# Two heads on the two column halves of TensorE: values held, probabilities streamed, and the division by the row sums put ahead of the transposes

## The chip, the cores and the metric

The kernel runs on one core of one Trainium2 chip. The metric is the device time of one execution in microseconds (us), where lower is better. The kernel before took 1848.61 us in the median of three runs (1846.76 to 1851.04).

## The reference, cut to what matters

The program is a stack of transformer layers on 256 tokens of width 1024: a mixer of stick-breaking and sparse attention ("even"), a conv-gated feed-forward layer, "forgetting" attention ("fox"), a second feed-forward layer, then a recurrent mixer and dilated attention ("dl") with feed-forward layers around them. All of it is float32. The change touches the last two products of the three attention stages. For fox, per head of width 64 and per block of 128 queries, they are:

```
s = jnp.einsum('bqhd,bshd->bhqs', qb, k, preferred_element_type=jnp.float32) * scale
s = s + (cq[..., :, None] - cum[..., None, :])
p = masked_softmax(s, kpos[None, :] <= tpos[:, None])
return jnp.einsum('bhqs,bshd->bqhd', p.astype(v.dtype), v)
```

The outputs of all 16 heads then stand side by side and are multiplied by an output matrix. In the sparse half of the even stage two such results (and a third over 15 compressed blocks) are added with a gate each; in the dilated stage three groups of keys share one softmax of 512 columns for each half of the tokens; in stick-breaking attention the weights come from a running product and aren't divided by a sum.

## The kernel before, in words

The three attention stages are the functions `even`, `fox` and `dilated`. Each projects its inputs with TensorE products of split operands (an fp32r high part and an fp32r low part, three products for each piece, lines 321 to 325), runs the heads in pairs, and multiplies the result by the output weights (`wout`). A pair of heads (j, with a = 0, 1) sits in one tile of 128 rows, head a in rows 64a to 64a+63.

The path of a pair, in fox: `scores` (line 555) makes the scores of both heads on TensorE, K = 64 rows each, head 0 in the upper and head 1 in the lower half of the rows. `softmax` takes the maximum (VectorE, lines 577 and 579) and the exponential with its row sum (ScalarE, line 594). `transpose_p` (line 598) turns the 128x128 blocks of probabilities on TensorE (line 604) into the PSUM tile `ps_PT`, and ScalarE copies them to the SBUF tile `PT` (line 606). `pv` (line 609) multiplies: the turned probabilities `PT` are the stationary operand (128x128), the values `v0`, `v1` (the two blocks of 128 keys) are the moving one (64 columns). The result `o` (`ps_o`) has queries on its partitions, two halves of tokens by two heads of 64 columns. `scale_out` (line 615) divides by the row sums while it copies `o` to `on` (line 622), and `heads_out` (line 625) turns `on` back with two TensorE transposes (line 630), because the output product wants channels on the partitions, and splits it into `oH` and `oL` (lines 634 and 635).

The even stage does the same without `scale_out`: its sparse half (`weigh` and `mix`, lines 809 and 824) has already scaled the probabilities (line 821), its stick-breaking half (`stick_a` and `stick_b`, lines 868 and 888) has nothing to divide by, and both copy `o` with ScalarE (lines 839 and 907). The dilated stage has its own `weigh` (line 1322) and `mix` (line 1346): per pair and half of the tokens, four blocks of keys for each head, so eight transposes (line 1351), two copies (line 1353) and eight products.

In the profile a float32 product stands as two MATMULs and two weight loads, called passes here; a transpose or an fp32r product is one. So the 200 products on `vN` and 48 on `vs` are 400 and 96 passes.

The order in which the stages ask for work is written out in the strings EVD, FXD and DLD (`w` weighs a pair, `m` mixes it; `x` and `y` in the even stage). Within that, the tile framework's scheduler gives each engine a fixed order when the kernel is built, and fills TensorE's gaps with projection products (`g` pieces, all named `ps_mm`). TensorE works through its list in that order. The scores have two PSUM banks (three in dl), the turned probabilities two, `o` one.

Of the kernel before, what the change touches and what calls it, by code (L numbers as in the profile page):

```python
# [9 lines left out]
F32 = mybir.dt.float32  # L10
# [3 lines left out]
AF = mybir.ActivationFunctionType  # L14
ALU = mybir.AluOpType
AX = mybir.AxisListType
P = 128
# [178 lines left out]
class Net:  # L196
# [411 lines left out]

    def pv(self, o, v0, v1, PT, first):

        k = {"skip_group_check": True}
        self.mm(o[:, 1], PT[:, 256:384], v0, start=first, stop=False, **k)
        self.mm(o[:, 1], PT[:, 0:128], v1, start=False, **k)
        self.mm(o[:, 0], PT[:, 128:256], v0, start=False, **k)

    def scale_out(self, o, sm, H, L, rev=False):
        nc = self.nc
        rs = self.sp.tile([P, 2, 2], F32, name="rs2")
        nc.vector.reciprocal(rs[:], sm[:])
        on = self.ap.tile([P, 2, P], F32, name="on")  # L620
        v = lambda z: z.rearrange("p t (a d) -> p (t a) d", d=64)
        nc.vector.tensor_mul(v(on[:]), v(o), rs[:].rearrange("p t a -> p (t a)")[:, :, None].to_broadcast([P, 4, 64]))
        self.heads_out(on, H, L, rev)

    def heads_out(self, on, H, L, rev=False):

        nc = self.nc
        p = self.psum((P, T), "PT")
        for tt in range(2):
            nc.tensor.transpose(p[:, tt * P:(tt + 1) * P], on[:, tt], self.ident[:])  # L630
        if rev:
            H, L = (z.rearrange("p (n t) -> p t n", t=2)[:, :, ::-1] for z in (H, L))
            p = p.rearrange("p (t n) -> p t n", t=2)
        nc.scalar.copy(H, p)
        nc.vector.tensor_sub(L, p, H.bitcast(F32))


    def even(self, done):
        nc, tc = self.nc, self.tc
        with ExitStack() as ctx:  # L640
# [168 lines left out]
            def weigh(j, b):  # L809

                rows = [slice(64 * a, 64 * a + 64) for a in range(2)]
                Sl = self.scores([qr[j // 2][r, j % 2, :] for r in rows], [kkr[r, b, :] for r in rows])
                sm = self.sp.tile([P, 2, 2], F32, name="sm2")
                ABs = self.softmax(Sl, [K["cmask"], K["cmask"]], 0.125, sm)
                rs = self.sp.tile([P, 2, 2], F32, name="rs2")
                nc.vector.reciprocal(rs[:], sm[:])
                nc.vector.tensor_mul(rs[:], rs[:], gview[:, :, j::4, 1 + b])
                for a in range(2):
                    for tt in range(2):
                        v = ABs[a][1 - tt]  # L820
                        nc.vector.tensor_scalar(v, v, rs[:, tt, a:a + 1], None, ALU.mult)
                NS[j, b] = ABs

            def mix(j, b):
                if b == 0:
                    NO[0] = self.psum((P, 2, P), "o")
                o, ABs = NO[0], NS.pop((j, b))
                for a in range(2):
                    PT = self.transpose_p(ABs[a])
                    s = slice(128 * b + 64 * a, 128 * b + 64 * a + 64)  # L830
                    self.pv(o[:, :, 64 * a:64 * a + 64], vs[:, 0, s], vs[:, 1, s], PT, a + b == 0)
                if b == 0:
                    return
                rr = slice(64 * (j % 2), 64 * (j % 2) + 64)
                for tt in range(2):
# [51 lines left out]

            def stick_b(u, j, a):
                utri, nones = K["utri"], K["nones"]
                if a == 0:  # L890
                    NO[0] = self.psum((P, 2, P), "o")
                o = NO[0]
# [6 lines left out]
                aT = ap.tile([P, 384], F32, name="PT", bufs=4)  # L899
                nc.scalar.activation(aT[:], Zv, AF.Exp)  # L900
                h = slice((2 * j + a) * 64, (2 * j + a) * 64 + 64)
                self.pv(o[:, :, 64 * a:64 * a + 64], vN[:, 0, h], vN[:, 1, h], aT, a == 0)
                if a == 0:
                    return
                c = 2 * u + j
                on = ap.tile([P, 2, P], F32, name="on")
                nc.scalar.copy(on[:], o)
                self.heads_out(on, oH[:, c, :], oL[:, c, :])

            E = {}  # L910
            qr = [None, None]
# [32 lines left out]
    def fox(self, done):  # L944
        nc, tc = self.nc, self.tc
        with ExitStack() as ctx:
# [40 lines left out]
            def weigh(u, j, qT, kT, e):  # L987
# [7 lines left out]
                e[:] = [self.softmax(Sl, [cmask, cmask], 0.125, sm), sm]  # L995

            def mix(u, j, vN, e):
                ABs, sm = e
                o = self.psum((P, 2, P), "o")
                for a in range(2):  # L1000
                    PT = self.transpose_p(ABs[a])
# [240 lines left out]
    def dilated(self, kH, kL, Rkv, done):  # L1242
        nc, tc = self.nc, self.tc
        with ExitStack() as ctx:
# [77 lines left out]
            def weigh(u, G, bias, j, t, sm):  # L1322

                two = lambda z: z.rearrange("p (b n) -> p b n", b=2)
                S = [self.psum((P, 512), "S") for _ in range(2)]
                for g, c, n in ((0, 0, 256), (1, 256, P), (2, 384, P)):
                    for a in range(2):
                        q, k = (G[g][i][64 * a:64 * a + 64, j, :] for i in range(2))
                        self.mm(S[a][:, c:c + n], q[:, t * P:t * P + P], k if g == 0 else k[:, t * P:t * P + P])
                Pt = ap.tile([P, 2, 512], F32, name="Pt")  # L1330
# [8 lines left out]
                                                       ALU.max, mx[:, a, i:i + 1])  # L1339
                nm = self.sp.tile([P, 2], F32, name="nmj")  # L1340
                nc.vector.tensor_reduce(nm[:], mx[:], AX.X, ALU.max, negate=True)
                for a in range(2):
                    nc.scalar.activation(Pt[:, a], Pt[:, a], AF.Exp, bias=nm[:, a:a + 1], accum_out=sm[:, t, a:a + 1])
                return Pt

            def mix(v, Pt, j, t, o):
                for a in range(2):
                    s = slice((2 * j + a) * 64, (2 * j + a) * 64 + 64)
                    pp = self.psum((P, 4, P), "PT")
                    for i in range(4):  # L1350
                        nc.tensor.transpose(pp[:, i], Pt[:, a, i * P:(i + 1) * P], self.ident[:])  # L1351
                    PT = ap.tile([P, 4, P], F32, name="PT", bufs=3)
                    nc.scalar.copy(PT[:], pp)
                    for i, val in enumerate((v[0][:, 0, s], v[0][:, 1, s], v[1][:, t, s], v[2][:, t, s])):
                        self.mm(o[:, t, 64 * a:64 * a + 64], PT[:, i], val, start=a + t + i == 0, stop=False,
                                skip_group_check=True)

            B = {}
            its, heads = DLD.split(), True
            for i, it in enumerate(its):  # L1360
# [15 lines left out]
                    B[("T",) + w] = turn(B.pop(("r",) + w), w[1])  # L1376
                elif n == "w":
                    u, jj, t = w
                    if t == 0:
                        B["m", u, jj] = self.sp.tile([P, 2, 2], F32, name="sm2")  # L1380
                    G = [B["T", u, g] for g in range(3)]
                    B[("p",) + w] = weigh(u, G, B["b", u], jj, t, B["m", u, jj])
                else:
                    u, jj, t = w
                    if t == 0:
                        o = self.psum((P, 2, P), "o")
                    mix([B["v", u, g] for g in range(3)], B.pop(("p",) + w), jj, t, o)
                    if t == 1:
                        self.scale_out(o, B["m", u, jj], oH[:, 2 * u + jj, :], oL[:, 2 * u + jj, :], rev=True)
            self.wout("dl", oH, oL, done)  # L1390

    def bias_scratch(self, cp, R=None):
# [201 lines left out]
```

## Time and profile before

| what | value |
|---|---|
| median of three runs | 1848.61 us |
| the profiled execution | 1848.29 us |
| its span, from the first to the last instruction | 1846.5 us |
| TensorE busy, share of the span | 99% |
| VectorE busy | 69% |
| ScalarE busy | 56% |
| granted TensorE clock, mean | 0.998 |

The profile is of one execution; a line number in it is that of the kernel file above. PE is TensorE's matmuls, PEld its weight loads, DVE is VectorE, ACT is ScalarE. [...]

### The profile page before, as it was taken

What the parts mean: (1) busy time and instruction counts of PE and PEld (TensorE: products, weight loads), DVE (VectorE), ACT (ScalarE), POOL (GpSimd) and SP (SyncE); (2) the same over time, 40 slices, a digit from 0 to 9 for tenths busy, and PEclk for the clock granted to TensorE, in tenths of its full rate; (3) what the DMA queues carried; (4) which work ended last, traced back from release to release, by engine and by line L of the source; (5) the groups of instructions that cost most, each with busy time, mean ns of one, the idle gap of its engine ahead of it and who ended that gap; (6) DMA issues with size and microseconds to landing.
All of it is one profiled execution on the core that took longest, in us unless ns stands there. A gap on an engine that the chain in (4) does not pass through costs nothing.

```text
span 1846.5 us, 37819 instructions
## 1 busy us (share of the span) xinstructions
PE 1826.5 (99%) x15709; PEld 1792.6 (97%) x15709; DVE 1268.5 (69%) x2695; ACT 1041.6 (56%) x2167; POOL 3.9 (0%) x18
## 2 busy tenths in 40 slices
PE   8999999999999999999999999999999999999999
PEld 7989999999999999999999999999999999999999
DVE  6557986654888687668988766866666456458763
ACT  5556665555666565556766554645456556556542
POOL 0000000000000000000000000000000000000000
PEclk9999999999999999999999999999999999999999
DMA  7313555641565546554335555555564434426553
GB/s 251 120 41 137 199 204 192 192 148 61 184 221 197 196 171 218 180 207 167 119 111 197 208 191 190 202 191 192 189 219 143 165 124 151 138 92 218 194 188 109
DMA packets 61160, 314.72 MB, mean 170 GB/s; under 512 B 10459, under 2 KB 21115, under 8 KB 28348
## 3 DMA queue, kind: packets, MB, share of 16 engines
q1 hardware_dynamic: 45792, 305.16, 46.7%
q10 hardware_dynamic: 15196, 7.15, 1.4%
q8 instruction: 123, 2.02, 0.4%
q14 instruction: 49, 0.40, 0.1%
HBM read 311.17 MB, written 1.11 MB: 169 GB/s over the span
## 4 chain that ended last, share of the span: by engine, by line
PE 95%; DVE 2%; ACT 1%; DMA 1%; issue 0%; SPq 0%; ACTq 0%
PE ps_mm L321 21%; PE ps_mm L324 21%; PE ps_mm L325 21%; PE ps_mm L293 6%; PE ps_mm L292 6%; PE ps_mm L294 6%; PE ps_S L332 4%; PE ps_o L332 4%; DMA raw<-in_wall_dram 1%; PE ps_PT L1351 1%; DVE wL L274 1%; PE ps_PT L332 1%; PE ps_PT L604 0%; PE ps_PT L1298 0%; ACT wH L273 0%; PE ps_PT L630 0%
## 5 line engine op out<-in xcount | busy, mean ns | idle before, releaser
L273 ACT CAST wH<-raw 128x512 fp32r<-128x512 f32 (+1 forms) x1212 | 651.5, 598 | 499.9 <-PE ps_mm L324 232.8
L274 DVE TENSOR_TENSOR wL<-raw,wH 128x512 fp32r<-128x512 f32 (+1 forms) x1212 | 755.4, 663 | 253.4 <-ACT wH L273 251.6
L321 PE MATMUL ps_mm<-xH,wH 128*128 128x256 f32 x2568 | 713.1, 278 | 8.8 <-ACT xH L343 7.0
L325 PE MATMUL ps_mm<-xH,wL 128*128 128x256 f32 x2560 | 711.7, 278 | 0.0
L324 PE MATMUL ps_mm<-xL,wH 128*128 128x256 f32 x2560 | 710.8, 278 | 0.2
L321 PEld LDWEIGHTS ps_mm<-xH,wH 128*128 128x128 f32 x2568 | 483.8, 189 | 10.5 <-ACT xH L343 7.0
L324 PEld LDWEIGHTS ps_mm<-xL,wH 128*128 128x128 f32 x2560 | 482.8, 189 | 0.8 <-DVE xL L344 0.7
L325 PEld LDWEIGHTS ps_mm<-xH,wL 128*128 128x128 f32 x2560 | 482.7, 189 | 0.7 <-DVE wL L274 0.3
L294 PE MATMUL ps_mm<-hH,wL 128*128 128x256 f32 x1056 | 291.5, 276 | 0.0
L292 PE MATMUL ps_mm<-hH,wH 128*128 128x256 f32 x1056 | 291.5, 276 | 0.0
L293 PE MATMUL ps_mm<-hL,wH 128*128 128x256 f32 x1056 | 291.5, 276 | 0.0
L293 PEld LDWEIGHTS ps_mm<-hL,wH 128*128 128x128 f32 x1056 | 198.2, 188 | 0.0
L294 PEld LDWEIGHTS ps_mm<-hH,wL 128*128 128x128 f32 x1056 | 198.2, 188 | 0.0
L292 PEld LDWEIGHTS ps_mm<-hH,wH 128*128 128x128 f32 x1056 | 198.2, 188 | 0.0
L321 PE MATMUL ps_mm<-wH,kH 128*128 128x256 f32 (+1 forms) x390 | 108.1, 279 | 0.0
L324 PE MATMUL ps_mm<-wL,kH 128*128 128x256 f32 x384 | 107.2, 279 | 0.0
L325 PE MATMUL ps_mm<-wH,kL 128*128 128x256 f32 x384 | 106.7, 278 | 0.0
L321 PE MATMUL ps_mm<-wH,xH 128*128 128x256 f32 (+1 forms) x372 | 104.2, 282 | 0.0
L324 PE MATMUL ps_mm<-wL,xH 128*128 128x256 f32 x368 | 103.5, 281 | 0.0
L325 PE MATMUL ps_mm<-wH,xL 128*128 128x256 f32 x368 | 103.4, 281 | 0.0
L503 DVE TENSOR_TENSOR t<-ps_mm,R 128x512 f32<-128x512 f32 x66 | 45.5, 690 | 74.1 <-PE ps_mm L325 74.0
L321 PEld LDWEIGHTS ps_mm<-wH,kH 128*128 128x128 f32 x390 | 72.9, 188 | 0.0
(295 smaller groups left out, 2247.9 us busy)
## 6 DMA issues: line engine op xcount, KB each, us to landing
raw<-in_wall_dram SPq DMA_DIRECT2D x254, 1024.0 KB, 4.8
raw<-in_wall_dram SPq DMA_DIRECT2D x40, 768.0 KB, 4.3
raw<-in_wall_dram SPq DMA_DIRECT2D x8, 512.0 KB, 3.3
bt<-scr ACTq DMA_DIRECT2D x8, 258.0 KB, 5.6
bt<-scr ACTq DMA_DIRECT2D x4, 512.0 KB, 6.7
x<-in_xin_dram SPq DMA_DIRECT2D x4, 256.0 KB, 5.4
raw<-in_wall_dram SPq DMA_DIRECT2D x4, 256.0 KB, 5.6
cw<-in_cmpw_dram ACTq DMA_DIRECT2D x1, 1024.0 KB
```

The source lines that it names most:

```text
L273: self.nc.scalar.copy(H[:, s], raw[:, s])
L274: self.nc.vector.tensor_sub(L[:, s], raw[:, s], H[:, s].bitcast(F32))
L292: nc.tensor.matmul(out, A[0], B[0], start=start, stop=False)
L293: nc.tensor.matmul(out, A[0], B[1], start=False, stop=False)
L294: nc.tensor.matmul(out, A[1], B[0], start=False, stop=stop)
L321: nc.tensor.matmul(out[:, j, at:at + n], A[0], B[0][:, at:at + n], start=c == c0 and j == 0, stop=False, **k)
L324: nc.tensor.matmul(out[:, j, :], A[0], B[1], start=False, stop=False, **k)
L325: nc.tensor.matmul(out[:, j, :], A[1], B[0], start=False, stop=c == c1 - 1, **k)
L332: self.nc.tensor.matmul(out, l, r, start=start, stop=stop, **k)
L503: nc.vector.tensor_mul(t2[:], u, Rb)
L1351: nc.tensor.transpose(pp[:, i], Pt[:, a, i * P:(i + 1) * P], self.ident[:])
```

## The change

`pv` swaps the operands: the values of one head (128 keys by 64 columns) are now stationary, and the turned probabilities (256 or 128 queries) move. The result `o` has channels on its partitions, head 0 on partitions 0 to 63 and head 1 on 64 to 127, so that the two heads use the two halves of TensorE's columns, and their products stand alternately in the program. `o` needs no turning back: `scale_out` and `heads_out` go, and `pair_out` splits `o` straight into `oH` and `oL`. Queries are no longer on the partitions of `o`, so the division by the sums moves to the probabilities: `scaled` in fox (four VectorE operations for each pair), two operations and a reciprocal of its own for each `weigh` in dl. `mix` turns both heads before it multiplies. In the scores the second head is asked first.

```diff
     def scores(self, q, k, extra=None):
...
-            for a in range(2):
+            for a in (1, 0):
                 self.mm(S[a][:, c:c + n], q[a][:, t], k[a][:, 0:n], stop=extra is None)
...
     def pv(self, o, v0, v1, PT, first):
 
         k = {"skip_group_check": True}
-        self.mm(o[:, 1], PT[:, 256:384], v0, start=first, stop=False, **k)
-        self.mm(o[:, 1], PT[:, 0:128], v1, start=False, **k)
-        self.mm(o[:, 0], PT[:, 128:256], v0, start=False, **k)
-
-    def scale_out(self, o, sm, H, L, rev=False):
+        for v, t, c in ((v0, slice(0, 256), slice(128, 384)), (v1, slice(128, 256), slice(0, 128))):
+            for a in range(2):
+                self.mm(o[64 * a:64 * a + 64, t], v[a], PT[a][:, c], start=first and v is v0, stop=False, **k)
+
+    def scaled(self, ABs, rs):
+        for a, AB in enumerate(ABs):
+            for tt in range(2):
+                v = AB[1 - tt]
+                self.nc.vector.tensor_scalar(v, v, rs[:, tt, a:a + 1], None, ALU.mult)
+
+    def pair_out(self, p, H, L, rev=False):
         nc = self.nc
-        rs = self.sp.tile([P, 2, 2], F32, name="rs2")
-        nc.vector.reciprocal(rs[:], sm[:])
-        on = self.ap.tile([P, 2, P], F32, name="on")
-        v = lambda z: z.rearrange("p t (a d) -> p (t a) d", d=64)
-        nc.vector.tensor_mul(v(on[:]), v(o), rs[:].rearrange("p t a -> p (t a)")[:, :, None].to_broadcast([P, 4, 64]))
-        self.heads_out(on, H, L, rev)
-
-    def heads_out(self, on, H, L, rev=False):
-
-        nc = self.nc
-        p = self.psum((P, T), "PT")
-        for tt in range(2):
-            nc.tensor.transpose(p[:, tt * P:(tt + 1) * P], on[:, tt], self.ident[:])
...
             def mix(j, b):
...
                 rr = slice(64 * (j % 2), 64 * (j % 2) + 64)
-                for tt in range(2):
-                    self.mm(o[:, tt], PcT[rr, j // 2, tt * P:(tt + 1) * P], vcz[rr, :], start=False,
-                            skip_group_check=True)
-                on = ap.tile([P, 2, P], F32, name="on")
-                nc.scalar.copy(on[:], o)
-                self.heads_out(on, oH[:, 4 + j, :], oL[:, 4 + j, :])
+                self.mm(o, vcz[rr, :], PcT[rr, j // 2, :], start=False, skip_group_check=True)
+                self.pair_out(o, oH[:, 4 + j, :], oL[:, 4 + j, :])
...
             def mix(u, j, vN, e):
-                ABs, sm = e
-                o = self.psum((P, 2, P), "o")
-                for a in range(2):
-                    PT = self.transpose_p(ABs[a])
-                    s = slice((2 * j + a) * 64, (2 * j + a) * 64 + 64)
-                    self.pv(o[:, :, 64 * a:64 * a + 64], vN[:, 0, s], vN[:, 1, s], PT, a == 0)
-                self.scale_out(o, sm, oH[:, 2 * u + j, :], oL[:, 2 * u + j, :])
+                o = self.psum((P, T), "o")
+                PT = [self.transpose_p(AB) for AB in e]
+                s = [slice((2 * j + a) * 64, (2 * j + a) * 64 + 64) for a in range(2)]
+                self.pv(o, *([vN[:, t, x] for x in s] for t in range(2)), PT, True)
+                self.pair_out(o, oH[:, 2 * u + j, :], oL[:, 2 * u + j, :])
...
             def weigh(u, G, bias, j, t):
...
+                sm, rs = (self.sp.tile([P, 2], F32, name=n) for n in ("smj", "rsj"))
                 for a in range(2):
-                    nc.scalar.activation(Pt[:, a], Pt[:, a], AF.Exp, bias=nm[:, a:a + 1], accum_out=sm[:, t, a:a + 1])
+                    nc.scalar.activation(Pt[:, a], Pt[:, a], AF.Exp, bias=nm[:, a:a + 1], accum_out=sm[:, a:a + 1])
+                nc.vector.reciprocal(rs[:], sm[:])
+                for a in range(2):
+                    nc.vector.tensor_scalar(Pt[:, a], Pt[:, a], rs[:, a:a + 1], None, ALU.mult)
                 return Pt
 
             def mix(v, Pt, j, t, o):
+                PTs = []
                 for a in range(2):
-                    s = slice((2 * j + a) * 64, (2 * j + a) * 64 + 64)
...
                     nc.scalar.copy(PT[:], pp)
-                    for i, val in enumerate((v[0][:, 0, s], v[0][:, 1, s], v[1][:, t, s], v[2][:, t, s])):
-                        self.mm(o[:, t, 64 * a:64 * a + 64], PT[:, i], val, start=a + t + i == 0, stop=False,
-                                skip_group_check=True)
+                    PTs.append(PT)
+                for i, val in enumerate((v[0][:, 0], v[0][:, 1], v[1][:, t], v[2][:, t])):
+                    for a in range(2):
+                        self.mm(o[64 * a:64 * a + 64, t * P:t * P + P], val[:, (2 * j + a) * 64:(2 * j + a) * 64 + 64],
+                                PTs[a][:, i], start=t + i == 0, stop=False, skip_group_check=True)
```

The stick-breaking half (`stick_b`) keeps the weights of head 0 until those of head 1 are there and then calls the same `pv` and `pair_out`.

TensorE's list at the first two pairs of fox, before. The rows stand one below another in the list; `ps_S` are scores, `c_ident` marks a transpose, `on` is the copied result.

```order
L604 MATMUL ps_PT<-c_ident,Pt_4635 128x128 x6
L321 MATMUL ps_mm<-wH,xH 128x256
L324 MATMUL ps_mm<-wL,xH 128x256
L332 MATMUL ps_o<-vN,PT 128x64 x6
L332 MATMUL ps_S<-kT,qT 128x256 x2
L332 MATMUL ps_S<-CF,selr 128x256 x2
L332 MATMUL ps_S<-kT,qT 128x128
L630 MATMUL ps_PT<-c_ident,on 128x128 x2
L332 MATMUL ps_S<-kT,qT 128x128
L332 MATMUL ps_S<-CF,selr 128x128 x2
```

The same place of the changed kernel.

```order
L604 MATMUL ps_PT<-c_ident,Pt_4567 128x128 x6
L321 MATMUL ps_mm<-wH,xH 128x256
L324 MATMUL ps_mm<-wL,xH 128x256
L332 MATMUL ps_o<-PT,vN 64x256 x2
L332 MATMUL ps_o<-PT,vN 64x128 x2
L332 MATMUL ps_S<-kT,qT 128x256 x2
L332 MATMUL ps_S<-CF,selr 128x256 x2
L332 MATMUL ps_S<-kT,qT 128x128 x2
L332 MATMUL ps_S<-CF,selr 128x128 x2
```

Six products of 64 columns became four of 256 and 128 columns on half of the array's columns, and the two transposes that cut the scores in two are gone.

TensorE's list in the first group of heads of dl, before.

```order
L332 MATMUL ps_o<-vN,PT 128x64 x4
L332 MATMUL ps_S<-k,qT 128x128
L332 MATMUL ps_S<-k,qT 128x256
L1351 MATMUL ps_PT<-c_ident,Pt 128x128 x2
L332 MATMUL ps_o<-vN,PT 128x64 x4
L1351 MATMUL ps_PT<-c_ident,Pt 128x128 x6
L332 MATMUL ps_S<-k,qT 128x256
L332 MATMUL ps_o<-vN,PT 128x64 x8
L332 MATMUL ps_S<-k,qT 128x128 x4
L630 MATMUL ps_PT<-c_ident,on 128x128 x2
```

The same group of the changed kernel, from the last scores ahead of the first transposes on.

```order
L332 MATMUL ps_S<-k,qT 128x256
L332 MATMUL ps_S<-k,qT 128x128 x2
L1337 MATMUL ps_PT<-c_ident,Pt 128x128 x8
L325 MATMUL ps_mm<-wH,xL 128x256
L321 MATMUL ps_mm<-wH,xH 128x128 x2
L332 MATMUL ps_o<-PT,vN 64x128
L324 MATMUL ps_mm<-wL,xH 128x256
L332 MATMUL ps_o<-PT,vN 64x128 x7
L1337 MATMUL ps_PT<-c_ident,Pt 128x128 x4
```

All scores of three `weigh` calls stand ahead of the first transposes now, and a product of full width stands between the first half-width product of a `mix` and its other seven.

VectorE's list for the first `weigh` in fox, before and, below it, changed; `nm` is the negated maximum, `Pt` the probabilities, `rs` the reciprocal of their sums `sm`.

```order
L579 ISA mx_4636 128x1
L274 TENSOR_TENSOR wL<-raw,wH 128x512
L591 TENSOR_SCALAR nm_4641<-mx_4636 128x4
L619 RECIPROCAL rs_4815<-sm_4634 128x4
L1014 TENSOR_TENSOR kT<-ps_mm,R 128x512
```

```order
L579 ISA mx_4568 128x1
L274 TENSOR_TENSOR wL<-raw,wH 128x512
L591 TENSOR_SCALAR nm_4573<-mx_4568 128x4
L978 RECIPROCAL rs_4579<-sm_4566 128x4
L620 TENSOR_SCALAR Pt_4567<-Pt_4567,rs_4579 128x128
L620 TENSOR_SCALAR Pt_4567<-Pt_4567,rs_4579 128x256
L620 TENSOR_SCALAR Pt_4567<-Pt_4567,rs_4579 128x128
L620 TENSOR_SCALAR Pt_4567<-Pt_4567,rs_4579 128x256
L996 TENSOR_TENSOR kT<-ps_mm,R 128x512
```

The transposes of this pair now wait for the four new operations, which stand behind the exponentials.

## Rows read from the trace of the kernel before

**Rows 1.** The page: span, busy time of each engine; the chain that ended last
```profile
span 1846.5 us, 37819 instructions
PE 1826.5 (99%) x15709; PEld 1792.6 (97%) x15709; DVE 1268.5 (69%) x2695; ACT 1041.6 (56%) x2167; POOL 3.9 (0%) x18
...
PE 95%; DVE 2%; ACT 1%; DMA 1%; issue 0%; SPq 0%; ACTq 0%
```

**Rows 2.** Windows: even, heads of fox, first head group of dl; busy us (instructions), clock
```profile
44.00:156.00 112.00, 111.46 (x867) 100.30 (x867) 63.75 (x213) 60.36 (x175) 0.00 (x0) 0.97 0.22 76
398.00:450.00 52.00, 51.23 (x420) 46.31 (x419) 25.36 (x94) 27.55 (x88) 0.00 (x0) 1.00 0.21 72
1412.00:1440.00 28.00, 27.47 (x223) 24.54 (x222) 13.27 (x57) 18.54 (x42) 0.00 (x0) 1.00 0.34 112
```

**Rows 3.** Groups by line and shape: operation xcount, busy us, mean ns, idle before
```profile
L332 PE MATMUL ps_o<-vN,PT 128*128 128x64 f32 x400 | 51.7, 277 | 1.0 <-ACT PT L606 0.5
L332 PE MATMUL ps_o<-vs,PT 128*128 128x64 f32 x96 | 12.6, 273 | 0.1
L630 PE MATMUL ps_PT<-c_ident,on 128*128 128x128 f32 x48 | 9.9, 288 | 0.5 <-ACT on L839 0.5
L332 PE MATMUL ps_o<-vcz,PcT 64*128 64x128 f32 x16 | 2.8, 297 | 0.0
```

**Rows 4.** Timeline of PE in dl: start us, length us, instruction, columns held, moving shape, count
```profile
1629.60 1.50 PE L332 MATMUL ps_o<-vN,PT 128*128 128x64 f32 x12
1630.94 0.61 PE L1351 MATMUL ps_PT<-c_ident,Pt 128*128 128x128 f32 x4
1631.47 0.72 PE L332 MATMUL ps_S<-k,qT 64*128 64x128 f32 x8
1632.12 0.39 PE L324 MATMUL ps_mm<-oL,wH 128*128 128x256 f32 x1
1632.34 1.04 PE L332 MATMUL ps_o<-vN,PT 128*128 128x64 f32 x8
...
1633.39 0.28 PE L321 MATMUL ps_mm<-oH,wH 128*128 128x256 f32 x1
1633.51 0.28 PE L324 MATMUL ps_mm<-oL,wH 128*128 128x256 f32 x1
```

**Rows 5.** Timeline of PE in the even stage
```profile
67.70 0.59 PE L332 MATMUL ps_S<-sb_sp,c_utri 128*128 128x256 f32 x2
68.14 0.39 PE L332 MATMUL ps_S<-sb_sp,nones 128*128 128x128 f32 x2
68.36 0.39 PE L332 MATMUL ps_S<-sb_sp,c_utri 128*128 128x128 f32 x2
68.65 1.13 PE L332 MATMUL ps_PT<-rp_s,c_rot 128*128 128x512 f32 x2
69.71 3.90 PE L332 MATMUL ps_PT<-cw,kx 128*32 128x64 f32 x64
```

**Rows 6.** The same, asked for 69 to 70 us alone
```profile
69.71 0.50 PE L332 MATMUL ps_PT<-cw,kx 128*32 128x64 f32 x5
```

**Rows 7.** Timeline of PE in fox, around the first transposes of `on`
```profile
405.24 0.38 PE L332 MATMUL ps_S<-kT,qT 64*128 64x128 f32 x2
405.55 0.44 PE L630 MATMUL ps_PT<-c_ident,on 128*128 128x128 f32 x2
405.92 0.37 PE L332 MATMUL ps_S<-kT,qT 64*128 64x128 f32 x1
```

**Rows 8.** Groups by line and shape, on DVE and ACT
```profile
L1343 ACT ACTIVATE Pt<-Pt,nmj 128x512 f32<-128x512 f32 x32 | 22.8, 715 | 5.5 <-DVE nmj L1341 3.7 <-issue 1.8
L622 DVE TENSOR_TENSOR on<-ps_o,rs 128x256 f32<-128x256 f32 x16 | 6.8, 424 | 20.1 <-PE ps_o L332 20.0
L1343 ACT ACTIVATION_READ_ACCUMULATOR Pt<-Pt,nmj 128x1 f32 x32 | 6.1, 189 | 0.0
L821 DVE TENSOR_SCALAR Pt<-Pt,rs 128x256 f32<-128x256 f32 x16 | 5.6, 347 | 0.0
L821 DVE TENSOR_SCALAR Pt<-Pt,rs 128x128 f32<-128x128 f32 x16 | 4.5, 282 | 0.1
L619 DVE RECIPROCAL rs<-sm 128x4 f32<-128x4 f32 x16 | 2.6, 173 | 20.7 <-ACT Pt L1343 10.4 <-ACT Pt L594 10.3
```

**Rows 9.** Waits: engine and line waited for, us in total, times, longest
```profile
PEld ps_PT L1351 <- ACT Pt L1343: 1.7, 5, 0.3
...
PE ps_PT L630 <- ACT on L839: 0.5, 2, 0.2
```

More of the change, by code (lines that the diff above doesn't have):

```diff
@@ L559, in scores @@
         for c, n, t in ((0, 256, slice(128, 256)), (256, 128, slice(0, 128))):
-            for a in range(2):
+            for a in (1, 0):
                 self.mm(S[a][:, c:c + n], q[a][:, t], k[a][:, 0:n], stop=extra is None)
-            for a in range(2):
+            for a in (1, 0):
                 if extra is not None:
@@ L817, in weigh @@
                 nc.vector.tensor_mul(rs[:], rs[:], gview[:, :, j::4, 1 + b])
-                for a in range(2):
-                    for tt in range(2):
-                        v = ABs[a][1 - tt]
-                        nc.vector.tensor_scalar(v, v, rs[:, tt, a:a + 1], None, ALU.mult)
+                self.scaled(ABs, rs)
                 NS[j, b] = ABs
@@ L825, in mix @@
                 if b == 0:
-                    NO[0] = self.psum((P, 2, P), "o")
+                    NO[0] = self.psum((P, T), "o")
                 o, ABs = NO[0], NS.pop((j, b))
-                for a in range(2):
-                    PT = self.transpose_p(ABs[a])
-                    s = slice(128 * b + 64 * a, 128 * b + 64 * a + 64)
-                    self.pv(o[:, :, 64 * a:64 * a + 64], vs[:, 0, s], vs[:, 1, s], PT, a + b == 0)
+                PT = [self.transpose_p(AB) for AB in ABs]
+                v0, v1 = ([vs[:, i, 128 * b + 64 * a:128 * b + 64 * a + 64] for a in range(2)] for i in range(2))
+                self.pv(o, v0, v1, PT, b == 0)
                 if b == 0:
@@ L898, in stick_b @@
                 self.mm(Z[:, 128:256], utri[:], sp[:, 0:128], start=False, stop=True, skip_group_check=True)
-                aT = ap.tile([P, 384], F32, name="PT", bufs=4)
+                aT = SB["p", a] = ap.tile([P, 384], F32, name="PT", bufs=4)
                 nc.scalar.activation(aT[:], Zv, AF.Exp)
-                h = slice((2 * j + a) * 64, (2 * j + a) * 64 + 64)
-                self.pv(o[:, :, 64 * a:64 * a + 64], vN[:, 0, h], vN[:, 1, h], aT, a == 0)
                 if a == 0:
                     return
+                o = self.psum((P, T), "o")
+                h = [slice((2 * j + i) * 64, (2 * j + i) * 64 + 64) for i in range(2)]
+                self.pv(o, *([vN[:, t, x] for x in h] for t in range(2)), [SB["p", i] for i in range(2)], True)
                 c = 2 * u + j
-                on = ap.tile([P, 2, P], F32, name="on")
-                nc.scalar.copy(on[:], o)
-                self.heads_out(on, oH[:, c, :], oL[:, c, :])
+                self.pair_out(o, oH[:, c, :], oL[:, c, :])
             E = {}
@@ L994, in weigh @@
                 sm = self.sp.tile([P, 2, 2], F32, name="sm2")
-                e[:] = [self.softmax(Sl, [cmask, cmask], 0.125, sm), sm]
+                e[:] = self.softmax(Sl, [cmask, cmask], 0.125, sm)
+                rs = self.sp.tile([P, 2, 2], F32, name="rs2")
+                nc.vector.reciprocal(rs[:], sm[:])
+                self.scaled(e, rs)
             def mix(u, j, vN, e):
-                ABs, sm = e
-                o = self.psum((P, 2, P), "o")
-                for a in range(2):
-                    PT = self.transpose_p(ABs[a])
-                    s = slice((2 * j + a) * 64, (2 * j + a) * 64 + 64)
-                    self.pv(o[:, :, 64 * a:64 * a + 64], vN[:, 0, s], vN[:, 1, s], PT, a == 0)
-                self.scale_out(o, sm, oH[:, 2 * u + j, :], oL[:, 2 * u + j, :])
+                o = self.psum((P, T), "o")
+                PT = [self.transpose_p(AB) for AB in e]
+                s = [slice((2 * j + a) * 64, (2 * j + a) * 64 + 64) for a in range(2)]
+                self.pv(o, *([vN[:, t, x] for x in s] for t in range(2)), PT, True)
+                self.pair_out(o, oH[:, 2 * u + j, :], oL[:, 2 * u + j, :])
             B = {}
@@ L1320, in biases, with weigh @@
                 return b0, b1
-            def weigh(u, G, bias, j, t, sm):
+            def weigh(u, G, bias, j, t):
                 two = lambda z: z.rearrange("p (b n) -> p b n", b=2)
@@ L1326, in weigh @@
                 for g, c, n in ((0, 0, 256), (1, 256, P), (2, 384, P)):
-                    for a in range(2):
+                    for a in (1, 0):
                         q, k = (G[g][i][64 * a:64 * a + 64, j, :] for i in range(2))
@@ L1341, in weigh @@
                 nc.vector.tensor_reduce(nm[:], mx[:], AX.X, ALU.max, negate=True)
+                sm, rs = (self.sp.tile([P, 2], F32, name=n) for n in ("smj", "rsj"))
                 for a in range(2):
-                    nc.scalar.activation(Pt[:, a], Pt[:, a], AF.Exp, bias=nm[:, a:a + 1], accum_out=sm[:, t, a:a + 1])
+                    nc.scalar.activation(Pt[:, a], Pt[:, a], AF.Exp, bias=nm[:, a:a + 1], accum_out=sm[:, a:a + 1])
+                nc.vector.reciprocal(rs[:], sm[:])
+                for a in range(2):
+                    nc.vector.tensor_scalar(Pt[:, a], Pt[:, a], rs[:, a:a + 1], None, ALU.mult)
                 return Pt
             def mix(v, Pt, j, t, o):
+                PTs = []
                 for a in range(2):
-                    s = slice((2 * j + a) * 64, (2 * j + a) * 64 + 64)
                     pp = self.psum((P, 4, P), "PT")
@@ L1378, in dilated @@
                     u, jj, t = w
[L1379 to L1380 removed]
                     G = [B["T", u, g] for g in range(3)]
[L1382 removed]
+                    B[("p",) + w] = weigh(u, G, B["b", u], jj, t)
                 else:
```

8 lines of the change are left out of this document (2 added, 6 removed).

## The prediction

> **What bounds the kernel now.** I read the page first: the span, the busy shares, and the chain of work that ended last. TensorE is busy for 1826.5 of 1846.5 us, and 95% of the chain is TensorE's own work [rows 1]; VectorE (69%) and ScalarE (56%) have room. [...] So the change is worth what it takes from or adds to TensorE's list, plus the waits that it makes there. The groups by line give the counts [rows 3], and the timeline the step from one end to the next, which is what an instruction really takes from the engine: the record of a product on `ps_o` lasts 277 ns, but eight of them end 0.87 us after the product ahead of them (1632.51 to 1633.38), and twelve in a row step by (1.50 - 0.28) / 11 = 0.111 us [rows 3, 4].
>
> **What the same timeline says of the array's shape.** Scores hold 64 rows; their neighbours hold 128. Transposes end at 1631.55 and the eight score passes behind them at 1632.19, that is 0.64 us. A pass of 128 float32 columns steps by 0.11 us and one of 256 by 0.22 (two of each end 0.22 and 0.44 us apart by their starts) [rows 5], so eight one after another would need 0.88: the two row halves overlap. Four overlapping pairs take 0.44, and 0.20 is left for entering the half-array shape. The projection product behind ends 0.32 us after the scores, where such products end 0.12 apart in a run: 0.20 for leaving [rows 4]. In fox, leaving to a transpose costs 0.37 - 0.22 = 0.15, and going back 0.30 - 0.11 = 0.19 [rows 7]. The only column-cut products of this kernel hold 32 columns: 59 of their 64 passes step by 0.058 us (70.21 to 73.61), and the first five end 0.43 us after their predecessor, which leaves 0.43 - 0.29 = 0.14 for entering [rows 5, 6]. So each change of shape costs 0.14 to 0.20 us of TensorE.
>
> **Removed.** 496 passes on `ps_o` (400 + 96) [rows 3] at 0.111 us: 55.1 us. 48 transposes of `on` at 0.11 (four take 0.45) [rows 4]: 5.3 us. With them goes TensorE's wait for `on`, 0.5 us [rows 3, 9], and eight copies on ScalarE and sixteen multiplications on VectorE, which cost nothing now, since both engines have room.
>
> **Added on TensorE, if the two heads overlap as the two row halves do.** A group of four products (fox 8 times, even 12 times: 4 stick-breaking pairs, 8 sparse ones) is two passes of 256 columns and two of 128 with the heads side by side: 2 x 0.22 + 2 x 0.11 = 0.66 us; 20 groups are 13.2. A dl `mix` is eight passes of 128 side by side, 0.88; sixteen are 14.1. But the list often puts other work between the first half-width product and the rest, and then that one has no partner: 8 groups of 20 (6 in even, 2 in fox) lose 0.44 each, all 16 of dl lose 0.22: 3.5 + 3.5. Sum 34.3 us. The product with `vcz` goes from two products of 128 columns to one of 256 for each of its four pairs: the same 0.44 us.
>
> **Changes of shape.** The half-width products are a third shape. I counted in TensorE's list the places where the shape changes to or from scores, `vcz` or the new products: 54 before and 78 after in even, 46 and 51 in fox (the transposes of `on` that cut scores in two are gone), 48 and 94 in dl. 75 more, at 0.14 to 0.20 us: 10.5 to 15.0. What a 64-column load costs at the entry no row shows; I take 0.17, between the 32-column entry and the 128-column one: 12.8 us.
>
> By stage, removed less added: even 16.0 - 10.5 + 1.8 - 4.1 = 3.2 us gained; fox 10.7 - 6.2 + 1.8 - 0.9 = 5.4; dl 28.4 - 17.6 + 1.8 - 7.8 = 4.8. Together 13.4.
>
> **The division ahead of the transposes.** In dl a reciprocal (0.173) and one operation on 512 columns (an estimate: 0.282 at 128 columns and 0.347 at 256 make 0.065 for each further 128, so 0.48) stand before the first transpose, and the reciprocal needs both heads' sums, so it also waits for the second exponential, 0.72 + 0.19: the first transposes can start about 1.5 us later than before [rows 8]. In fox it is the reciprocal moved forward and 2 x 0.347 + 2 x 0.282 = 1.26 us. VectorE's load rises by about 4 us in a window of 28 where it has 13, so it doesn't become the bound [rows 2]. Queued behind the new operations on VectorE are the next maxima, which free the score banks, and the low parts of the weights. What covers the latency is that the list has the scores of later pairs and projection products in between; where it can fail is the first `mix` of each of dl's four groups, where TensorE already waited for the exponentials (1.7 us in five waits) [rows 9]. The bounds are 0 and 1.5 us in each, 0 to 6; I take 0.5, 2.0 in all. Reversing the heads in the scores costs nothing that I can see: the same products in the same shape.
>
> **Sum.** -13.4 - 0.5 + 2.0 = -11.9 against the profiled execution's 1848.29 us, which is the median of the runs (1848.61) to 0.02%: 1836.4, so I predict 1836.
>
> **Rivals.**
> *The two column halves take turns.* No row shows two column halves at work; what overlaps in rows 4 are row halves, which read different partitions, while here both heads read all 128. In turns, a group takes 1.32 and a `mix` 1.76 us, 54.6 in all; the missing partners then cost nothing. Saved are 0.5 + 5.3 + 0.5, added 12.8 + 2.0: +8.5, 1857 us, slower. It decides once less than about a third of the overlap comes: that is worth 27 us when whole, and 9 of them pay for the changes of shape. For it speaks that nothing shows the contrary; against it that a product of 32 columns is so much cheaper to load and that the row halves do overlap.
>
> [...]
> [...]
>
> *The halves overlap in part.* Two loads for each pair of passes have to go through before the next; a product of 64 columns steps by 0.111 now, which its columns alone (half of 128) do not explain, so there the 128-column load sets the step [rows 4, 5]. If a 64-column load took more than half of that, the dl pairs would step by more than 0.11: at 0.15, 128 pairs lose 5 us, and 80 pairs of the others some 2: 1843.
> [...]
>
> *The division comes to stand on the path.* If the list doesn't cover it, 16 times 1.1 us in dl (0.17 + 2 x 0.48) and 8 times 1.4 in fox are 29 us; half of it is 14.5, and the gain is gone: 1849. For it: TensorE's list is fixed, and one late transpose holds all behind it. Against it: VectorE is half idle there [rows 2], and in fox several pairs of scores and some 40 projection products stand between.
>
> *Shape changes are cheaper.* A 64-column entry nearer 0.10 and transposes behind it at 0.15 would give 75 x 0.12 = 9, and no new waits: 1830.
>
> **Chances.** The forecast 0.58 with its own range 1831 to 1841; cheaper changes 0.10 (1827 to 1831); partial overlap 0.13 (1841 to 1846); the division on the path 0.09 (1843 to 1855); halves in turn 0.08 (1852 to 1860); bare loads 0.02 (1852 to 1862). The range for 8 in 10 runs from 1828 to 1847. A measurement of this kernel can tell about 0.2%, 3.7 us, from no change. Faster by more: the first two, nearly all of the third and a little of the fourth, 0.80. Within it: 0.08. Slower: 0.12.
>
> **What would show it.** In the profile after: two half-width products of one pair starting a few ns apart and ending together, and a group of four taking about 0.66 us, a `mix` of dl 0.88; if it takes 1.3 or 1.8, the halves take turns. The first product of full width behind such a group should end some 0.2 us later than in a run. No rows of `on` in fox, dl and even. The stretches of [rows 2] should be shorter by about 3 us (even), 5 (fox), and 0.7 us in each dl group. New waits of TensorE's loads for VectorE's `Pt` in dl should sum to 2 us; if they come to 10 or more, the division is on the path, and my cover was wrong. Projection and feed-forward products should keep their step; if the granted clock falls there or in the heads, something that I left out is at work.

## The result, and the profile after

The changed kernel took 1835.07 us in the median (1834.62 to 1835.77, four runs), the kernel before on the same chip 1847.89 (1846.76 to 1851.04). The ratio is 0.9928, with a 95% interval of 0.9911 to 0.9945: 0.7% faster, where 1836 was forecast. On another chip five more runs of it gave 1836.82 beside 1848.81, ratio 0.9931 (0.9917 to 0.9944).

The page after: span and busy times, and the shares of the chain that ended last, as in [rows 1].

```profile
span 1832.8 us, 37608 instructions
PE 1812.0 (99%) x15573; PEld 1762.6 (96%) x15573; DVE 1283.1 (70%) x2751; ACT 1038.9 (57%) x2159; POOL 3.9 (0%) x18
...
PE 93%; DVE 3%; DMA 2%; ACT 1%; issue 0%; SPq 0%; ACTq 0%
```

TensorE still sets the time. Its busy time fell by 14.5 us, the span by 13.7; VectorE got 14.6 us more to do; what that cost TensorE the experiments show.

The groups after by line and shape, which answer to [rows 3] and [rows 8]: operation, count, busy us, mean ns, idle time before them.

```profile
L332 PE MATMUL ps_o<-PT,vN 128*64 128x128 f32 x304 | 33.3, 282 | 0.4 <-ACT PT L1339 0.3
...
L1337 PE MATMUL ps_PT<-c_ident,Pt 128*128 128x128 f32 x128 | 18.7, 280 | 0.3 <-DVE Pt L1329 0.3
...
L604 PE MATMUL ps_PT<-c_ident,Pt 128*128 128x128 f32 x96 | 14.7, 279 | 2.0 <-DVE Pt L620 1.8
...
L1329 DVE TENSOR_SCALAR Pt<-Pt,rsj 128x512 f32<-128x512 f32 x32 | 14.2, 480 | 0.2
...
L332 PE MATMUL ps_o<-PT,vN 128*64 128x256 f32 x48 | 13.4, 405 | 0.7 <-ACT PT L606 0.5
...
L620 DVE TENSOR_SCALAR Pt<-Pt,rs 128x256 f32<-128x256 f32 x32 | 11.1, 347 | 0.0
...
L620 DVE TENSOR_SCALAR Pt<-Pt,rs 128x128 f32<-128x128 f32 x32 | 9.0, 282 | 0.4
...
L332 PE MATMUL ps_o<-PT,vs 128*64 128x256 f32 x32 | 7.5, 405 | 0.0
...
L332 PE MATMUL ps_o<-PT,vs 128*64 128x128 f32 x32 | 5.0, 276 | 0.0
```

496 passes on `ps_o` became 416, each with 64 columns held, and no row names `on` in these stages any more. The dividing operation on 512 columns takes 0.480 us, as estimated. Its transposes (L1337) wait 0.3 us for it, those of fox and even (L604) 1.8, of it 1.5 in fox.

TensorE's timeline after, in dl: start us, length us, instruction, columns held, moving shape, count.

```profile
1411.71 0.39 PE L324 MATMUL ps_mm<-wL,xH 128*128 128x256 f32 x1
1412.02 1.09 PE L332 MATMUL ps_o<-PT,vN 128*64 128x128 f32 x14
1413.04 0.66 PE L1337 MATMUL ps_PT<-c_ident,Pt 128*128 128x128 f32 x4
...
1414.13 0.28 PE L324 MATMUL ps_mm<-wL,xH 128*128 128x256 f32 x1
1414.37 0.43 PE L332 MATMUL ps_o<-PT,vN 128*64 128x128 f32 x2
1414.74 0.39 PE L325 MATMUL ps_mm<-wH,xL 128*128 128x256 f32 x1
```

The same, asked for 1412.02 to 1412.06 alone:

```profile
1412.02 0.33 PE L332 MATMUL ps_o<-PT,vN 128*64 128x128 f32 x2
```

Two passes begin within 0.01 us of each other: the column halves work side by side. Fourteen passes (six pairs and two without a partner) end 1.01 us after the projection product ahead (1412.10 to 1413.11). Eight steps of 0.109 are 0.87, so 0.14 went into entering the new shape. Four transposes behind them end 0.59 later, 0.15 more than their 0.44: leaving it. At 1414.37 stand the two passes of the product without a partner, cut off from its `mix` by a projection product: it pays both changes for 0.22 us of work.

For the time by stage I take the ends of the feed-forward layers' output products as marks. Between them lie four stretches that vary; all others agree to 0.02 us in every kernel, but for 0.23 at the end of one. All in us, from one profiled execution each; the columns right of "after" are of the experiments below.

| stretch | before | after | after, again | no division | late head first | one half |
|---|---|---|---|---|---|---|
| even, and the feed-forward's input | 291.03 | 285.60 | 288.32 | 288.98 | 285.53 | 281.53 |
| fox, and the feed-forward's input | 246.99 | 243.81 | 242.72 | 240.77 | 240.66 | 245.87 |
| recurrent mixer (not changed) | 270.35 | 268.79 | 270.21 | 269.69 | 269.13 | 269.30 |
| dl, and the feed-forward's input | 433.89 | 430.37 | 430.64 | 428.35 | 422.71 | 436.61 |

Even gained 5.4, fox 3.2 and dl 3.5 us; 1.6 came from a stretch that the change doesn't touch. How much one execution differs from the next has to be known before the first row is read, and a part of it is the clock. Windows of the kernel before: us, busy time (instructions) of PE, PEld, DVE, ACT and POOL, granted clock, DMA share, GB/s.

```profile
20.00:36.00 16.00, 16.00 (x139) 15.71 (x138) 10.68 (x20) 7.47 (x15) 0.00 (x0) 1.00 0.79 286
...
44.00:46.00 2.00, 2.00 (x10) 1.76 (x10) 1.43 (x5) 0.24 (x1) 0.00 (x0) 0.50 0.00 0
...
48.00:50.00 2.00, 2.00 (x11) 2.00 (x11) 0.98 (x2) 1.60 (x5) 0.00 (x0) 0.50 0.86 365
...
44.00:52.00 8.00, 8.00 (x40) 7.20 (x40) 4.03 (x9) 3.81 (x8) 0.00 (x0) 0.59 0.36 131
```

The windows of the same stretch and of [rows 2] after:

```profile
44.00:52.00 8.00, 7.82 (x61) 7.10 (x61) 6.37 (x14) 6.62 (x15) 0.00 (x0) 1.00 0.37 136
44.00:156.00 112.00, 111.35 (x842) 92.17 (x842) 68.03 (x222) 60.99 (x174) 0.00 (x0) 1.00 0.24 84
398.00:450.00 52.00, 49.57 (x407) 42.79 (x406) 31.84 (x128) 29.86 (x98) 0.00 (x0) 1.00 0.20 67
```

And of the changed kernel's second profile:

```profile
44.00:52.00 8.00, 8.00 (x37) 7.03 (x37) 3.21 (x7) 3.67 (x8) 0.00 (x0) 0.57 0.36 131
```

In the profile of before the granted clock went down to 0.50 for some 7 us at the start of the even stage, after a stretch in which TensorE was busy without a gap (24.00 of 24 us from 20 to 44). The 0.97 in [rows 2] was this. In the first profile after it stayed at 1.00 there, in the second it fell at the same place (0.57 from 44 to 52 us). Of the other columns of the table, "no division" and "late head first" have the fall too (0.97 from 44 to 156 us, as in the profile of before, and 0.57 from 44 to 52 us), while "one half" has not (1.00 from 44 to 52). So in the row of even, before compares with "after, again" and these two, and "after" with "one half". With the fall in both, even went from 291.03 to 288.32, a gain of 2.7 us; the other 2.7 is the clock's. So at like clock the change gains 2.7 in even, 3.2 to 4.3 in fox and 3.3 to 3.5 in dl: 9 to 10.5 us in these profiles, against medians that lie 12 to 13 apart. The clock doesn't close that gap: on the second chip, executions of the two kernels with the same mean granted clock (0.997, 0.998 or 0.999) differ by 11.3 to 12.3 us in their means, against 10.4 between the two profiles with the fall. Where the other 1 to 2 us lie, these profiles don't show.

In fox a row of 49.57 busy of 52 us, where [rows 2] had 51.23, shows new gaps. The timeline after has one of them:

```profile
406.47 0.98 PE L604 MATMUL ps_PT<-c_ident,Pt 128*128 128x128 f32 x6 [0.57 <-DVE Pt L620]
407.38 0.38 PE L332 MATMUL ps_S<-CF,selr 64*128 64x256 f32 x2
407.69 1.19 PE L332 MATMUL ps_o<-PT,vN 128*64 128x256 f32 x8
```

The first transpose waits 0.57 us for the division. The eight passes behind the scores are one group of four products; they end 1.12 us after the scores (407.76 to 408.88), where 0.66 and 0.15 for the entry make 0.81. By the single records head 1's first pass starts 0.33 us after head 0's: its turned probabilities come later, and for that long a half of the columns is idle.

### The profile page after: what moved, and what is told of

It reads as the page before. It is cut to its first block, busy times and chain, and to the rows that moved or that the text cites. A ratio compares the mean times of both kernels' runs of the same rounds, so it can differ in the third digit from the quotient of the medians.

```text
span 1832.8 us, 37608 instructions
## 1 busy us (share of the span) xinstructions
PE 1812.0 (99%) x15573; PEld 1762.6 (96%) x15573; DVE 1283.1 (70%) x2751; ACT 1038.9 (57%) x2159; POOL 3.9 (0%) x18
## 4 chain that ended last, share of the span: by engine, by line
PE 93%; DVE 3%; DMA 2%; ACT 1%; issue 0%; SPq 0%; ACTq 0%
PE ps_mm L321 21%; PE ps_mm L325 21%; PE ps_mm L324 21%; PE ps_mm L292 7%; PE ps_mm L293 7%; PE ps_mm L294 7%; PE ps_S L332 4%; PE ps_o L332 3%; DMA raw<-in_wall_dram 2%; DVE wL L274 1%; PE ps_PT L1337 1%; PE ps_PT L604 1%; PE ps_PT L332 0%; PE ps_PT L1280 0%; ACT wH L273 0%
```

## The experiments

All edits are against the changed kernel, or, where it says so, against the version with the late head first. The first four ran on one chip, where before took 1849.36 us, the other three on a second, where it took 1848.81.

**One head after the other.** The same products, head 0's all ahead of head 1's:

```diff
-        for v, t, c in (...):
-            for a in range(2):
+        for a in range(2):
+            for v, t, c in (...):
...
-                for i, val in enumerate(...):
-                    for a in range(2):
+                for a in range(2):
+                    for i, val in enumerate(...):
```

> The changed kernel with one edit: all products of head 0 stand ahead of all of head 1, instead of alternately (pv and the mix of dl). Theory A (the gain comes of two neighbouring products in the list that go to different column halves; TensorE begins its products in the order of the list): a product of head 0 behind another of head 0 waits for it, and head 1 is held up behind it, so a group of four takes 1.07 us instead of 0.64 and a mix of dl 1.5 instead of 0.86; with 20 groups and 16 mixes that is +18.8 us, less about 10 that the list saves because it cuts fewer groups into pieces (shape changes in dl fall from 94 to 69): about 1843. Theory B (each column half has a queue of its own and runs ahead by itself): the order inside a group doesn't matter, and the fewer shape changes alone show: about 1826.

Measured: 1839.4 us (1837.11 to 1840.78), ratio 0.995 (0.9933 to 0.9966). The timeline of its first `mix` in dl:

```profile
1413.09 1.58 PE L332 MATMUL ps_o<-PT,vN 128*64 128x128 f32 x16
```

Sixteen passes as eight pairs would make a record of 1.09 us, one after another 1.96 (both seen below). Here it is 1.58, neither: by the single records head 1's first pass starts beside the fifth of head 0's eight (1413.580 and 1413.575), and from there the halves overlap. It is the same in all 14 `mix` calls of dl that the list leaves whole: head 1's first pass starts 0.49 us after head 0's. So the order of the products matters here, and alternating them is what makes the overlap whole (1.09 us for 1.58), but the two halves overlapped without strict alternation too (1.58 for 1.96). It also means that the sentence in the description of the kernel, by which TensorE works through its list in that order, didn't hold here between the two halves: this pass starts ahead of three passes of head 0 that stand in front of it in the list. The time lies between the two theories: dl's products take 22.6 us for 17.4, and 25 changes of shape fewer there (69 for 94) give 4.5 of that back.

**No division.** This version leaves out the reciprocals and multiplications of fox and dl, so its attention outputs are not divided:

```diff
-                rs = self.sp.tile([P, 2, 2], F32, name="rs2")
-                nc.vector.reciprocal(rs[:], sm[:])
-                self.scaled(e, rs)
...
-                nc.vector.reciprocal(rs[:], sm[:])
-                for a in range(2):
-                    nc.vector.tensor_scalar(Pt[:, a], Pt[:, a], rs[:, a:a + 1], None, ALU.mult)
```

> The changed kernel without the division: the reciprocals and the multiplications of the probabilities by them are left out in fox and in dl (the output isn't divided by the sums). Theory A (the division stands on the path in fox, where TensorE's transposes wait 1.8 us for it, and is covered in dl): fox gets about 2 us shorter, dl stays within 1 us: 1832 to 1834. Theory B (the division is covered everywhere, and fox fell short of its forecast for the shape changes alone): no change, 1835. Theory C (the division costs much in both): 1825 or less.

Measured: 1833.11 us (1828.81 to 1835.99), ratio 0.9911 (0.9892 to 0.993). The interval overlaps that of the changed kernel (0.9911 to 0.9945), so the medians alone don't tell the two apart, and what follows is read from the stretches of one profile. Fox is 2.0 to 3.0 us shorter than in the two profiles of the changed kernel, dl 2.0 to 2.3. Theory A had the total and fox; that dl would move by more than 1 us it didn't say. The group of fox's transposes in this version:

```profile
L604 PE MATMUL ps_PT<-c_ident,Pt 128*128 128x128 f32 x96 | 15.4, 280 | 0.9 <-ACT Pt L594 0.3 <-DVE Pt L620 0.3
```

The waits for `Pt` on L620 that are left are those of the even stage; fox's 1.5 us are gone, and with them some of what stood around them. In dl the list of TensorE changed too (99 changes of shape, 94 before), so there the 2.0 are the price of the division with its effect on the order, not of waits alone.

**Scores with head 0 first again.**

```diff
     def scores(self, q, k, extra=None):
...
-            for a in (1, 0):
+            for a in range(2):
```

with the same edit in the loop of the bias products behind it and in dl.

> The changed kernel with the scores asked in the old order, head 0 first. Theory A (the reversed order does nothing by itself; the list merely comes out a little differently, with 88 shape changes in dl instead of 94): 1833 to 1836. Theory B (the reversed order is needed so that the last scores to arrive are those whose maximum is taken last): VectorE starts later, and the time rises by 3 us or more, to 1838.

Measured: 1838.88 us (1835.59 to 1840.73), ratio 0.9942 (0.9925 to 0.996). The median lies where theory B put it and not within theory A's range, but its interval overlaps that of the changed kernel (0.9911 to 0.9945). The profile, which is of the fastest of the four executions (1835.59 us), has fox at 243.05 and dl at 430.12 us: within the 1.1 us by which the two profiles of the changed kernel differ in fox, and 0.25 to 0.5 under them in dl. So the stages show nothing that the reversed order buys; whether it is worth the 1.5 to 2.3 us by which this version gains less than the changed kernel stays open.

**The late head first.** Head 1's probabilities are ready last. With its product first in each pair, no product of head 0 goes ahead alone:

```diff
-            for a in range(2):
+            for a in (1, 0):
                 self.mm(o[64 * a:64 * a + 64, t], v[a], ...)
...
-                    for a in range(2):
+                    for a in (1, 0):
                         self.mm(o[64 * a:64 * a + 64, t * P:t * P + P], ...)
```

> The changed kernel with one edit: in each pair of products the one of head 1 comes first (pv and the mix of dl). Its turned probabilities come last, so no product starts before both heads are there, and the list no longer puts other work between the first half-width product and the rest: 24 lone products become 0, shape changes in dl fall from 94 to 60. Theory A (lone products and shape changes cost what the trace says, 0.43 or 0.21 us and about 0.17 us each): 8 x 0.43 + 16 x 0.21 + 38 x 0.17 = 13.3 us less, 1822. Theory B (the time before both heads are there is spent in any case, and TensorE now waits for the second copy instead of working on the first): within 3 us of the changed kernel, 1832 to 1838.

Measured: 1823.91 us (1823.09 to 1829.61), ratio 0.987 (0.9851 to 0.9889), which is theory A's 1822 and not B's 1832 to 1838. The profiled execution is the slowest of the four, with more falls of the granted clock (0.79 from 164 to 172 us, where before has 1.00; 0.996 in the mean of the span, where the profiled run on the second chip has 0.998), so the stretches and rows of this version are taken from its run on the second chip, below.

**The changed kernel again, and the late head first again.**

> The changed kernel once more, beside the two others on one chip. Both theories: 1835 us within 0.2%, fox about 243.8 and dl about 430.4 us in the marks used so far, since these two stretches differed by less than 0.8 us between executions.

Measured: 1836.82 us (1834.65 to 1839.34), ratio 0.9931 (0.9917 to 0.9944).

> The version with the late head first once more, on the same chip as the changed kernel. Theory A (the 34 shape changes fewer in dl and the missing partners are what it gains): 1824 to 1827, 8 to 11 us under the changed kernel, of it 7 to 8 in dl and 2 to 2.5 in fox. Theory B (the other chip, or the slack in the even stage, gave part of it): 4 us or less under it, with the stretches of fox and dl within 2 us of the changed kernel's.

Measured: 1823.88 us (1822.87 to 1825.92), ratio 0.9864 (0.9851 to 0.9878): 12.9 us under the changed kernel on the same chip, more than either theory said. Of it 7.9 are in dl, 2.1 in fox and 2.8 in even, at the same clock there (0.57 from 44 to 52 us in both). The timeline in dl, and the group of its products:

```profile
1408.63 0.28 PE L321 MATMUL ps_mm<-wH,xH 128*128 128x256 f32 x1
1408.94 1.09 PE L332 MATMUL ps_o<-PT,vN 128*64 128x128 f32 x16
1409.97 0.66 PE L1337 MATMUL ps_PT<-c_ident,Pt 128*128 128x128 f32 x4
```

```profile
L332 PE MATMUL ps_o<-PT,vN 128*64 128x128 f32 x304 | 22.2, 278 | 0.1
```

A whole `mix` stands together now, sixteen passes in 1.09 us of record. In dl the products take 14.05 us where the changed kernel took 17.42, and 60 changes of shape (12.4 us) are left of 94 (18.3): 5.9 us for 34, so 0.175 for each. This version beats both kernels.

**One half for both heads.** From the late head first, in fox and dl both heads use columns 0 to 63, head 1 into another part of the same bank; the copies of the result are split in two:

```diff
-                        self.mm(o[64 * a:64 * a + 64, t * P:t * P + P], ...)
+                        self.mm(o[0:64, 256 * a + t * P:256 * a + t * P + P], ...)
```

> As the version with the late head first, but in fox and dl both heads use columns 0 to 63, head 1 into another part of the same PSUM bank; loads, passes and their order stay, each copy of the result becomes two. Theory A (the gain of the change is that two column halves run side by side): every pair of passes takes twice its time, 8 x 0.65 = 5.2 us in fox and 16 x 0.88 = 14.1 in dl, 19.3 more than the version with the late head first, which is about 1843; the shape changes stay. Theory B (the products got cheaper because a load of 64 columns is short or the wide moving side spares loads, and the side-by-side is not needed): within 3 us of that version, about 1825.

Measured: 1843.41 us (1839.57 to 1846.48), ratio 0.9968 (0.9956 to 0.9979), 19.5 us over the late head first. The same place and group:

```profile
1410.03 0.28 PE L321 MATMUL ps_mm<-wH,xH 128*128 128x256 f32 x1
1410.34 1.96 PE L332 MATMUL ps_o<-PT,vN 128*64 128x128 f32 x16
1412.23 1.12 PE L1354 MATMUL ps_PT<-c_ident,Pt 128*128 128x128 f32 x8
```

```profile
L332 PE MATMUL ps_o<-PT,vN 128*64 128x128 f32 x304 | 37.8, 276 | 0.8 <-ACT PT L1356 0.6
```

The record grows from 1.09 to 1.96 us, by eight steps of 0.109. By the ends, dl's products take 27.92 us for 14.05, fox's 10.38 for 5.23: both 1.99 times. Even, which kept the two halves here, takes the same for its products in both versions, to 0.01 us. Theory A holds. The operands' exchange by itself buys little in the products: before, dl's took 29.2 us. What the change gains it gains from the two halves at work at once.

## Why the prediction was right, step by step

For each step I sum, over TensorE's products, each one's end less the latest end ahead of it (nothing if it ends earlier); where the shape changes, what goes beyond the step of a run is put to the change.

**The overlap** was the step on which all rested, and it holds. The forecast's 0.66 for a group of four is 0.654 measured (7.85 / 12 in even and 5.23 / 8 in fox, in the version without lone products), its 0.88 for a `mix` 14.05 / 16 = 0.878. The one-half version prices the first rival: in turn the products would take 27.9 (dl) + 10.4 (fox) + 15.7 (even, twice its 7.85) = 54.0 us, where I had 54.6, and the changed kernel took 36.7. That is 17.3 more, an estimate of 1852 us, slower than before.

**Bare loads**, that is loads whose time adds to that of the products, have a chance of 0.02 in the forecast (1852 to 1862); no run shows such a term. The loads of the new products use all 128 rows, and pairs of passes still step by 0.109 us, with two loads to each, where a full-width pass of 128 columns, with one load, steps by 0.11; so the loads don't show. The overlap in part didn't come either: where that rival has 0.15 us for a pair, the step is the same 0.109, and two halves gave 1.99 times the speed of one.

**Products and transposes.** Forecast were -55.1 + 34.3 = -20.8 us for the products and -5.3 for the transposes of `on`; measured -21.9 (even -5.1, fox -5.0, dl -11.8) and -5.6. Both sides of the first were a little low: the old products took 58.5, the new ones 36.7. Lone products cost 3.4 us in dl, where I had 3.5, but 6.2 in even and fox (19.2 less 13.1), where I had counted 3.5: there the second half also starts late where the list doesn't cut a product off, as in the group at 407.69.

**Changes of shape.** Forecast 75 more at 0.17, 12.8 us; measured +14.6 (even 3.2, fox 3.0, dl 8.3), waits that end at such a place among them. In dl alone, where there are few, 46 more cost 8.3: 0.18 each. The 64-column entry itself doesn't lie between those of the other shapes, as I had guessed: in the median it takes 0.14 us, as much as the 32-column one. The way out takes 0.15 to transposes and 0.19 to 0.20 to scores and full-width products, so the two together average near the 0.17 that I took; what came on top are waits.

**The division** is where terms of the forecast failed: its term for fox was put at nothing, and its term for dl came out in size but not in the place where I had put it. In fox I costed it at nothing, covered by scores of later pairs and projection products. The waits after say otherwise: us in total, times, longest.

```profile
PEld ps_PT L604 <- issue: 4.1, 10, 1.1
...
PEld ps_o L332 <- ACT PT L606: 3.6, 12, 0.7
...
PEld ps_o L332 <- issue: 2.4, 12, 0.3
...
PEld ps_o L332 <- ACT PT L1339: 2.3, 8, 0.5
...
PEld ps_PT L1337 <- issue: 2.2, 13, 0.2
...
PE ps_PT L604 <- DVE Pt L620: 1.8, 3, 0.9
...
PEld ps_PT L1337 <- DVE Pt L1329: 0.5, 1, 0.5
...
PE ps_PT L1337 <- DVE Pt L1329: 0.3, 1, 0.3
```

1.5 of the 1.8 us are in fox (the rest in even, where the line scaled before as well), and taking the division out gave 2.0 to 3.0 back (one profile against two). So fox gained 3.2 to 4.3 instead of 5.4; without the division it would have been 6.2. In dl I put 2.0 us of new waits at the first `mix` of each head group. The version without it is 2.0 to 2.3 faster there, but the 2 us of waits that I named as the sign aren't there: the trace names 0.5 us of the loads' waits for L1329 and 0.3 of the transposes'. The size was right, while the place was not shown. Scores (+1.1) and projections (+1.2) take more between the same marks than before, and without the division they fall back by 1.5 and 1.1, so it is spread along the list; by which waits stays open.

**Even** came out at 5.4 for a forecast of 3.2 and 0.5 for the wait on `on`; at like clock it is 2.7. A fall of the clock in the profile that I worked from was visible in its 0.97, and I didn't take it into account.

Together: forecast -11.9, the medians -12.8 and -12.0. The profiled spans differ by 13.7, of which 2.7 are the clock and 1.6 the recurrent mixer. The second profile, with the fall of the clock in it as before, stands at -10.4. The mechanism was right; that the sum lies so near owes something to offsets.

## What to carry to other kernels

Here two products that hold 64 columns each shared TensorE as two column halves at 1.99 times the speed of one half, where their instructions alternated and both had their operands (sixteen passes in 1.09 us of record for 1.96); the price was 0.14 to 0.20 us for each change of shape, so keep them in long runs. When two interleaved streams become ready at different times, ask for the late one first: a scheduler then has nothing to send ahead alone, and here that reversal of two loops was worth as much as the whole change (12.9 us beside 12.0). Before a stage's gain is read from two profiles, compare the granted clock of the same stretch in both.

## What the runs showed of the hardware

- Column halves that read the same 128 rows overlapped wholly in this float32 kernel: pairs of passes start 0.007 us apart by the single records and step by 0.109, no more than one full-width pass of 128 columns (0.11); in one half they took 1.99 times as long (27.92 us for 14.05 in dl).
- Where one half's eight passes all stood ahead of the other's, the second half started beside the fifth of them, 0.49 us after the first, ahead of three that stand in front of it in the list (all 14 whole `mix` calls of that version): 1.58 us for sixteen passes, between 1.09 and 1.96.
- The granted clock has a mean of 0.996 to 0.998 in seven of the nine profiles and of 1.000 in two, the first of the changed kernel and that of one half. In the profile of before it was 0.50 from 44 to 50 us; from 44 to 52 us it was 0.57 to 0.59 in before, the second of the changed kernel and both of the late head first, and 1.00 in the two, though in these as in before TensorE had been busy for all of the 24 us ahead (24.00 of 24 from 20 to 44 us). In the profile of before the fall costs 8 x 0.41 = 3.3 us of full-clock work in the window of 44 to 52 us. What decides on it these runs don't show.
